# A bidirectional RWKV-7 and short-convolution layer on one core: operands stored in pairs, one convolution group done later, and the inverse's blocks stored from another queue

## The chip, the core and the metric

The kernel runs on one core of a Trainium2 chip. The metric is device time in microseconds (us) of one execution; before the change it is 1746.37 us, the median of three runs (1745.83 to 1748.89).

## What is computed

One layer for 128 context tokens and 2048 latent tokens (2176 columns) of width 1024, all in fp32. Both kinds of token go through a modulated RMS norm `h`, one input projection to eight groups of 512 channels, a mixer with two halves, and an output projection with a residual:

```python
proj = h @ lp['w_in']
r, k, v, g_a, b_gate, c_gate, u_conv, g_b = jnp.split(proj, IN_SPLITS, axis=-1)
ya, s_final = _wkv(h, r, k, v, s0, lp)                     # 8 heads x 64, two directions
ya = ya.astype(x.dtype) * jax.nn.silu(g_a)
yb = b_gate * _short_conv(c_gate * u_conv, lp['conv_w'], is_latent) * jax.nn.silu(g_b)
u = jnp.concatenate([ya, yb], axis=-1) @ lp['w_out']
```

`_wkv` is the RWKV-7 recurrence with a decay and an in-context rate for each direction:

```python
s_kk = jnp.einsum('bdhij,bdhj->bdhi', S, kk_t)
S = (S * w_t[..., None, :] - s_kk[..., :, None] * (kk_t * a_t)[..., None, :]
     + v_t[..., :, None] * k_t[..., None, :])
return S, jnp.einsum('bdhij,bdhj->bdhi', S, r_t)
```

## The kernel before

**Engines.** TensorE (PE) multiplies, VectorE (DVE), ScalarE (ACT) and GpSimd (POOL) work element by element, and SyncE (SP) issues nearly all transfers. A value that two phases share lies in a scratch tensor in memory (`scr_...` in the profile). The program gives the order of the steps, and a scheduler of the compiler, which works with times of its own, settles the order of the instructions on each engine.

**Phase 1** (`phase1`, from L43) makes everything that needs the projection. The columns are cut into six blocks of 384 columns (the last has 256), taken two by two, in thirds (`THIRD`). fp32 is split into a high and a low part, so a product `dense` of one block with 128 output channels is 24 matmuls (L160 to L162). In each third a loop over four groups `g` of 128 channels (L626 to L628) calls `turn(0, g, ...)` and `turn(1, g, ...)`, and each turn does both blocks of the third:

- The first turn does `mixA`: the products for k and r, the token shift (`shifted`: L319 and L321 on ScalarE, L323 on POOL, L327 or L329 on VectorE), the norm of kk by a sum over partitions (`part_sum`: L196, L197, L204, L205), and for both directions the decay (tanh, L371, and a scan, L375 or L377) and the four operands of the recurrence: `al` (L387), `rh` (L390), `kap` (L398) and `be` (L401 and L402). Each operand is a tile of 128x384 from a ring of four places with the tag `sp`, and is stored at once by SyncE (`spill`, L335) to `ops0` or `ops1`. A place is free again when its store has landed. A last sum over the heads, `psb`, gives `bsum`.
- The second turn does `gateA`: v, its transpose, centred, in `vt` (one place, L425 and L432) and stored (L433); the gate sg (L439, stored); and `q` (L441 to L444), which takes a place of the ring `sp`.
- Beside them a turn can do half of a convolution group (`partB`): `convB` with the products c and u (`mmc`, `mmu`) and the taps, or `gateB` with the products gb and b. In the first two thirds group g is done in the turns of g. In the last third groups 0 and 1 are spread over the four first turns, and groups 2 and 3 come after all mix turns, interleaved with `K.early()`.

Weights come in by `load_w` (L119): first from the input through a ring of two tiles `wr` of 4 KB a partition (used in the first third only, when the split parts are also stored), later as split parts.

**Phase 2** (`phase2`, from L694) is the recurrence, in chunks of 64 tokens and 17 stages of 16 chunk-heads. A stage s has these parts: `partL` loads operands into `rr` (L868, SyncE); `partM` copies block-diagonal operands (`bd`, L779, ScalarE), makes the products psF, psG (L892) with masks, and cuts the 32x32 diagonal blocks `dg`, which are stored to `at` (L899, on ScalarE's queue); `partI` loads them in another layout (`ab`, L914), inverts them on POOL (L919 to L934) and stores `zt` (L935, POOL's queue); `partW` loads `str`, `stl`, `sv` and the inverses `zc`; `partU` transposes them (`zr`, L984, VectorE) and completes the inverse (psU L992, psW); `partB` makes psX (L1018) and psE (L1029), E on VectorE (L1030); `partS` is the serial chain of states (psS L1054, sv L1067). M and the inverse of a stage run three stages ahead (`LA`). `K.early()` is the setup (among it `presetR`, L787, which writes an identity into `rr`) and L, M and I of stages 0 and 1. `main()` starts behind phase 1: it does M and I of stage 2, U and B of stage 0, and then the loop over the stages, in which the parts of coming stages are placed between the eight steps of the serial chain.

**Phase 3** is the output projection (psu, L1287 to L1289), partly ahead of the recurrence's end.

Of the kernel before, what the change touches and what calls it, by code (L numbers as in the profile page):

```python
# [6 lines left out]
F32 = mybir.dt.float32  # L7
# [20 lines left out]

OPS = dict(al0=0, rh0=1, ka0=2, be0=3, be1=0, ka1=1, rh1=2, al1=3)


class Ctx:
# [15 lines left out]
def phase1(K):  # L50
# [3 lines left out]
    wp = Pool(K, "p1w", "left", 2)  # L54
# [58 lines left out]
                up[n, d] = (hi[:, n, d], lo[:, n, d])  # L113

    kept = set()

    def load_w(cb):

# [212 lines left out]

    def spill(name, g, j, t_, nm):
        t0, n = BLK[j]
        dst = S[f"ops{name[2]}"][OPS[name]] if name in OPS else S[name]
        nc.sync.dma_start(dst[g * 128:(g + 1) * 128, t0:t0 + n], t_[:, :n])  # L335

    def mixA(g, j, ws, hh, lw, pre):

# [19 lines left out]
        for d in range(2):  # L358
            cs = slice(g * 128, g * 128 + 128)

            def lup(which):
                ps = pmm.tile([128, 384], F32, tag="mm", name=f"up{which}_{K.u()}")
                hi, lo = up[which, d]
                x = lw[which * 2 + d]
                T.matmul(ps[:, :n], hi[:, cs], x[:, :n], start=True, stop=False)
                T.matmul(ps[:, :n], lo[:, cs], x[:, :n], start=False, stop=True)
                return ps

            psw = lup(0)
            t = tl("t", 2)  # L370
            P.activation(t[:, :n], psw[:, :n], AF.Tanh, bias=dcol(D_W0H + d * 4 + g), scale=0.5)  # L371
            V.tensor_scalar(t[:, :n], t[:, :n], -0.5 * DEC, -0.5 * DEC, ALU.mult, ALU.add)
            c = t
            if d == 0:
                V.tensor_tensor_scan(c[:, :n], smask[:, :n], t[:, :n], 0.0, ALU.mult, ALU.add)  # L375
            else:
                V.tensor_tensor_scan(c[:, :n][:, ::-1], smask[:, :n], t[:, :n][:, ::-1], 0.0, ALU.mult, ALU.add)  # L377
            pt = rot(pp[d], "pp")
            c3 = c[:, :n].rearrange("p (a b) -> p a b", b=64)
            P.activation(pt[:, :nch, 1 - d:65 - d], c3, AF.Exp)  # L380
            P.activation(c[:, :n], c[:, :n], AF.Exp, bias=nln2[:], scale=-1.0)
            psa = lup(1)
            ta = tl("ta", 2)
            P.activation(ta[:, :n], psa[:, :n], AF.Tanh, bias=dcol(D_IBH + d * 4 + g), scale=0.5)
            v3 = lambda x_: x_[:, :n].rearrange("p (a b) -> p a b", b=64)
            al = tl("sp", 4)
            V.tensor_tensor(v3(al), v3(kk), pt[:, :nch, d:64 + d], ALU.mult)  # L387
            spill(f"al{d}", g, j, al, "al")
            rh = tl("sp", 4)
            V.tensor_tensor(v3(rh), v3(rS), pt[:, :nch, 1 - d:65 - d], ALU.mult)  # L390
            spill(f"rh{d}", g, j, rh, "rh")
            nc.scalar.dma_start(S[f"pc{d}"][g * 128:(g + 1) * 128, t0 // 64:t0 // 64 + nch], pt[:, :nch, 64 - 64 * d])

            kd = tl("kd", 2)
            P.activation(kd[:, :n], ta[:, :n], AF.Identity, bias=dcol(D_KA2 + g), scale=vcol(V_KA + g))
            V.tensor_tensor(kd[:, :n], kd[:, :n], kS[:, :n], ALU.mult)
            kap = tl("sp", 4)
            V.tensor_tensor(kap[:, :n], kd[:, :n], c[:, :n], ALU.mult)  # L398
            spill(f"ka{d}", g, j, kap, "kap")
            be = tl("sp", 4)  # L400
            V.scalar_tensor_tensor(be[:, :n], ta[:, :n], 1.0, kkn[:, :n], ALU.add, ALU.mult)  # L401
            V.tensor_tensor(be[:, :n], be[:, :n], c[:, :n], ALU.mult)  # L402
            spill(f"be{d}", g, j, be, "be")
            kds.append(kd)
        bs = kds[0]
        V.tensor_tensor(bs[:, :n], kds[0][:, :n], kds[1][:, :n], ALU.add)
# [6 lines left out]
    def gateA(g, j, ws, hh, bsum):  # L413
# [6 lines left out]
        psv = pax.tile([128, 3, 128], F32, tag="ax", name=f"psv{g}_{j}")  # L420
        for i in range(n // 128):
            T.transpose(psv[:, i, :], vS[:, i * 128:(i + 1) * 128], idt[:])
        vt = ta_.tile([128, 3, 128], F32, tag="vt", name=f"vt{g}_{j}", bufs=1)

        c0 = 1 if lat_off(j) else 0  # L425
        if c0:
# [11 lines left out]
        sg = tg  # L438
        V.scalar_tensor_tensor(sg[:, :n], tg[:, :n], 1.0, psg[:, :n], ALU.add, ALU.mult)  # L439
        spill("sg", g, j, sg, "sg")  # L440
        q = tl("sp", 4)  # L441
        V.tensor_tensor(q[:, :n], bsum[:, :n], vS[:, :n], ALU.mult)
        V.scalar_tensor_tensor(q[:, :n], q[:, :n], dcol(D_GBH + g), sg[:, :n], ALU.add, ALU.mult)
        spill("q", g, j, q, "q")  # L444
# [126 lines left out]
    for t3, js in enumerate(THIRD):  # L571
        wd, wi = wlora if t3 == 0 else (load_w(32), load_w(33))
        lws, pre, conv, sums = {}, {}, {}, {}
        more = coming(*THIRD[t3 + 1]) if t3 < 2 else iter(())
        WA, WB = ((4, 0), (8, 12)), ((20, 24), (28, 16))
        early = gate_rows() if t3 == 0 else iter(())
# [10 lines left out]
        def turn(h, ga, gb):  # L587
# [5 lines left out]
            for j in js:  # L593
# [13 lines left out]
                if ga == 3 and h and j == js[0] and t3 < 2:  # L607
                    run(more)
                    j2 = THIRD[t3 + 1][1]
                    more = make_h(j2, xb[j2])  # L610
            if first:
                wb = [load_w(cb + gb[0]) for cb in WB[gb[1]]]
                for j in js:
                    partB(gb[0], j, gb[1], wb)
# [9 lines left out]
            prepare(js[1])  # L624
            load_up()
        for g in range(4):  # L626
            turn(0, g, (g, 0) if t3 < 2 else (g // 2, g % 2))
            turn(1, g, (g, 1) if t3 < 2 else None)  # L628
        run(more)
        if t3 == 2:  # L630
            for p in (pax, ta_, hr, ca):
                p.close()
            early = K.early()
            for g in (2, 3):
                for h in range(2):
                    wb = [load_w(cb + g) for cb in WB[h]]
                    for j in js:
# [53 lines left out]
def phase2(K):  # L691
# [179 lines left out]
    def partM(s, st):  # L871

        at = S["at"][s]
        for gi, g in enumerate(st.g):
# [20 lines left out]
            def blocks():  # L895
                dg = tl([128, 8, 32], "dg", 1, O.rI)
                P.activation(dg[:], g.GA[:, :, 64:96], AF.Identity, scale=B.hm[:, 0:1])
                V.scalar_tensor_tensor(dg[:], g.GA[:, :, 96:128], B.hm[:, 1:2], dg[:], ALU.mult, ALU.add)
                nc.scalar.dma_start(at[gi * 8:gi * 8 + 8].rearrange("u s b j i -> (s b j) u i"), dg[:])  # L899

            F = lambda h: product(h, g.F, pb, rr[:, 2:4], B.msk[:, MF[d]], "F")
            GA = lambda h: product(h, g.GA, qb, rr[:, 1::-1], B.mkg[:, MG[d]], "G")
# [511 lines left out]
```

## Time and profile before

| | before |
|---|---|
| median of the runs | 1746.37 us (1745.83 to 1748.89) |
| span of the profiled execution | 1752.9 us |
| busy: PE, PEld, DVE, ACT, POOL | 94%, 89%, 62%, 50%, 33% |
| mean of PE's granted clock in the first third, second third, third 3, recurrence | 0.97, 0.98, 1.00, 0.96 |
| moved by DMA | 335.69 MB, 192 GB/s |

The median is of runs of their own; the profile is of one execution, 6.5 us longer. All durations are from that one. In a row of a timeline stand the start in us, the duration in us, the engine, the line of the kernel, the operation, what it writes and reads, and in brackets how long its engine stood idle before it and what ended that. In a row of the waits stand the engine and its tile and line, what it waited for, the us in total, how many times, and the longest. "Landing" is the time from a transfer's issue to its end.

Phase 1 fills the span up to about 1000 us (the first third from 60, the second from 395, the third's mix turns from 720 to 935, its late conv groups to 1002), the recurrence runs to about 1505 us.

### The profile page before, as it was taken

Reading aid. Unit: us, or ns where it says so; the run is one execution under the profiler, and the core shown is the slowest. Engines: PE = TensorE matmul, PEld = TensorE weight load, DVE = VectorE, ACT = ScalarE, POOL = GpSimd, SP = SyncE. Lnnn points to the kernel's source line nnn. Section 1 sums busy time; section 2 is a strip of 40 time slices with the busy share of each in tenths; the row PEclk is TensorE's granted clock in tenths of the full one; section 3 lists DMA queues with packets and bytes.
Section 4 is the critical chain, followed back from the end, with each engine's and each line's share of the span. In section 5 each row is a group of like instructions: output and inputs, shape, how many; then the busy total and the mean of one; then the engine's idle time right before and its main releaser. Section 6 shows DMA issues by size and latency. Waiting matters only on the chain. (4 is left out here: it accounts for less than half of the span.)

```text
span 1752.9 us, 33041 instructions
## 1 busy us (share of the span) xinstructions
PE 1647.9 (94%) x12400; PEld 1558.8 (89%) x12400; DVE 1093.0 (62%) x2092; ACT 870.1 (50%) x1719; POOL 582.1 (33%) x1089
## 2 busy tenths in 40 slices
PE   5999899998999999999998989999999999899998
PEld 2889898998999998999998979899999999787886
DVE  5875788866567766567764544475776666656333
ACT  4534455534143433334442367687788787633222
POOL 0011111111011101011120587777777778223221
PEclk9899999999999999999999998899999999999999
DMA  9797778785557646477666585587677875746442
GB/s 367 208 234 220 233 241 246 232 255 151 148 160 227 169 147 174 135 258 217 195 214 225 173 196 135 141 192 187 174 198 189 191 185 120 180 151 206 151 144 90
DMA packets 315825, 335.69 MB, mean 192 GB/s; under 512 B 166985, under 2 KB 263881, under 8 KB 301585
## 3 DMA queue, kind: packets, MB, share of 16 engines
q1 hardware_dynamic: 243360, 324.52, 62.6%
q10 hardware_dynamic: 70944, 4.60, 2.9%
q0 software_dynamic: 1360, 4.46, 0.7%
q8 instruction: 98, 1.61, 0.4%
q14 instruction: 63, 0.51, 0.1%
HBM read 221.42 MB, written 112.08 MB: 190 GB/s over the span
## 5 line engine op out<-in xcount | busy, mean ns | idle before, releaser
L934 POOL TENSOR_TENSOR zt<-zt,ztmp 128x30 f32<-128x30 f32 (+7 forms) x510 | 197.3, 387 | 39.3
L1054 PE MATMUL psS<-sv,E 128*128 128x64 f32 x1088 | 155.1, 277 | 1.0 <-DVE sv L1067 0.6
L1029 PE MATMUL psE<-str,stl 128*128 128x128 f32 x1088 | 144.1, 281 | 11.3 <-DVE E L1030 7.0
L1054 PEld LDWEIGHTS psS<-sv,E 128*128 128x128 f32 x1088 | 145.4, 200 | 3.3 <-DVE sv L1067 0.8
L1029 PEld LDWEIGHTS psE<-str,stl 128*128 128x128 f32 x1088 | 131.8, 194 | 14.1 <-DVE E L1030 7.9
L931 POOL TENSOR_TENSOR ztmp<-ab,zt 128x60 f32<-128x60 f32 (+7 forms) x255 | 130.8, 513 | 19.2
L1067 DVE TENSOR_TENSOR sv<-psS,pc 64x128 f32<-64x128 f32 x254 | 69.2, 277 | 92.9 <-PE psS L1054 92.2
L779 ACT COPY bd<-rr 64x512 f32<-64x512 f32 x136 | 84.0, 617 | 75.7 <-DMA rr<-scr_ops 23.3
L323 POOL TENSOR_TENSOR shk<-rawl 128x384 f32<-128x384 f32 (+1 forms) x24 | 20.7, 861 | 291.9 <-ACT rawl L319 291.9
L1030 DVE TENSOR_TENSOR E<-psE,msk 128x512 f32<-128x512 f32 x136 | 92.7, 684 | 33.0 <-PE psE L1029 32.3
L892 PE MATMUL psF<-rr,bd 128*128 128x128 f32 x544 | 80.0, 295 | 16.2 <-ACT Q L779 9.8
L892 PEld LDWEIGHTS psF<-rr,bd 128*128 128x128 f32 x544 | 70.7, 203 | 20.4 <-ACT Q L779 12.9
L1350 POOL TENSOR_TENSOR z<-z,x 128x512 f32<-128x512 f32 x32 | 43.6, 1364 | 126.6 <-DVE z L1346 105.9
L1018 PE MATMUL psX<-F,zb 128*128 128x128 f32 x544 | 78.2, 297 | 3.2 <-ACT zb L777 2.3
L197 POOL TENSOR_TENSOR hslb<-kd,hshb 128x384 fp32r<-128x384 f32 (+1 forms) x24 | 26.7, 1113 | 164.0 <-ACT hshb L196 143.5
L160 PE MATMUL mmc<-h,w 128*128 128x384 f32 (+1 forms) x192 | 67.9, 354 | 13.4 <-ACT q1r L321 9.8
L323 POOL TENSOR_TENSOR shv<-rawl 128x384 f32<-128x384 f32 (+1 forms) x24 | 25.4, 1060 | 153.4 <-ACT rawl L319 153.4
L892 PE MATMUL psG<-rr,bd 128*128 128x128 f32 x544 | 72.0, 280 | 4.4 <-DVE F L893 4.4
L1018 PEld LDWEIGHTS psX<-F,zb 128*128 128x128 f32 x544 | 71.6, 209 | 4.0 <-POOL zt L934 1.9
L892 PEld LDWEIGHTS psG<-rr,bd 128*128 128x128 f32 x544 | 65.7, 193 | 5.0 <-DVE F L893 4.8
L161 PE MATMUL mmc<-h,w 128*128 128x384 f32 (+1 forms) x192 | 66.1, 344 | 0.0
L162 PE MATMUL mmc<-h,w 128*128 128x384 f32 (+1 forms) x192 | 65.7, 342 | 0.0
(307 smaller groups left out, 5205.4 us busy)
## 6 DMA issues: line engine op xcount, KB each, us to landing
w<-scr_wsp SPq DMA_DIRECT2D x68, 1024.0 KB, 7.3
scr_wsp<-w SPq DMA_DIRECT2D x34, 1024.0 KB, 6.0
rr<-scr_ops SPq DMA_DIRECT2D x64, 512.0 KB, 4.6
scr_ops<-sp SPq DMA_DIRECT2D x160, 192.0 KB, 5.2
wr<-in_win SPq DMA_DIRECT2D x34, 512.0 KB, 6.3
ab<-scr_at SPq DMA_DIRECT2D x34, 256.0 KB, 4.2
x<-in_x SPq DMA_DIRECT2D x17, 512.0 KB, 3.8
wadas<-in_wada SPq DMA_DIRECT2D x8, 1024.0 KB, 13.0
```

Of the source, the lines that this page charges most:

```text
L160: T.matmul(ps[:, :n], w[:, 0, k], hh[:, 0, k, :n], start=k == 0, stop=False)
L161: T.matmul(ps[:, :n], w[:, 0, k], hh[:, 1, k, :n], start=False, stop=False)
L162: T.matmul(ps[:, :n], w[:, 1, k], hh[:, 0, k, :n], start=False, stop=k == 7)
L779: (V.tensor_copy if k in ON_DVE else P.copy)(dst, src)
L892: T.matmul(ps[:, i, :].rearrange("p (a b) -> p a b", b=64), w[:, u, :], x[:, :, u, :], start=True, stop=True)
L931: G.tensor_tensor(tv, ab[:, j:j + 2, j + 2:32].unsqueeze(1).broadcast_to((128, kn, 2, n)), zt[:, :kn, j:j + 2].unsqueeze(3).broadcast_to(( ...
L934: G.tensor_tensor(zt[:, :kn, j + 2:32], zt[:, :kn, j + 2:32], tv[:, :, r], ALU.subtract)
L1018: T.matmul(px[:, i, :], B.zb[:, gi, us.start + i, :], g.F[:, us.start + i, :], start=True, stop=True)
L1029: T.matmul(pe[:, i, hd, :].rearrange("p (b t) -> p b t", b=2), g.lt[:, :, hd, us.start + k + i].rearrange("p b t -> p (b t)"), g.rt[:, :, ...
L1030: V.tensor_tensor(g.E[n][:, k:k + 2].rearrange("p a b c -> p (a b) c"), pe[:].rearrange("p a b c -> p (a b) c"), B.msk[:, ME[g.d]].unsquee ...
L1054: T.matmul(sp[gi][:, q, hd, :], g.E[n][:, k, hd, :], sv[:, u, hd, :], start=True, stop=True)
L1067: r = V.tensor_tensor(dst, sp[gi][0:64, q], B.pc[0:64, d, 2 * p:2 * p + 2, c:c + 1].broadcast_to((64, 2, 64)), ALU.mult)
```

## The change

It has four parts. The lines of the kernel after are 11 to 13 further on than those of before.

1. **Pairs.** `al` and `rh` are written into the two halves of one tile, `kap` and `be` into those of another, and each pair is stored by one transfer (`spill2`): 96 stores for 192. In the first third the pairs have two places in the room of the former four. From the second third on, when `wr` has no weights to hold any more, every other pair lies in `wr`: four pair places.
2. **q and vt.** `q` is computed in `bsum` and takes no operand place. From the second third on `vt` lies in `wr` too, with two places.
3. **Convolution.** In the last third only group 0 is done beside the mix turns, its halves at g = 1 and g = 3; the first turns of g = 0 and g = 2 have none. Group 1 is done behind the mix turns with 2 and 3, interleaved with `K.early()` (which ends the pools for the operands first).
4. **The inverse's blocks.** `dg` is stored by SyncE (`D` is `nc.sync.dma_start`) in place of ScalarE.

```diff
@@ spill, new pair() and spill2()
 def spill(name, g, j, t_, nm):
     t0, n = BLK[j]
-    dst = S[f"ops{name[2]}"][OPS[name]] if name in OPS else S[name]
-    nc.sync.dma_start(dst[g * 128:(g + 1) * 128, t0:t0 + n], t_[:, :n])
+    nc.sync.dma_start(S[name][g * 128:(g + 1) * 128, t0:t0 + n], t_[:, :n])
+npair = [0]
+def pair():
+    npair[0] += 1
+    nm = f"pair{npair[0]}"
+    if late and npair[0] % 2:
+        return wp.tile([128, 2, 384], F32, tag="wr", name=nm, bufs=2)
+    return ta_.tile([128, 2, 384], F32, tag="sp", name=nm, bufs=2)
+def spill2(d, k, g, j, t_):
+    t0, n = BLK[j]
+    nc.sync.dma_start(S[f"ops{d}"][k:k + 2, g * 128:(g + 1) * 128, t0:t0 + n].rearrange("k p t -> p k t"), t_[:, :, :n])
@@ mixA
-al = tl("sp", 4)
+ar = pair()
+al, rh = ar[:, d], ar[:, 1 - d]
 V.tensor_tensor(v3(al), v3(kk), pt[:, :nch, d:64 + d], ALU.mult)
-spill(f"al{d}", g, j, al, "al")
-rh = tl("sp", 4)
 V.tensor_tensor(v3(rh), v3(rS), pt[:, :nch, 1 - d:65 - d], ALU.mult)
-spill(f"rh{d}", g, j, rh, "rh")
+spill2(d, 2 * d, g, j, ar)
...
-kap = tl("sp", 4)
+kb = pair()
+kap, be = kb[:, d], kb[:, 1 - d]
 V.tensor_tensor(kap[:, :n], kd[:, :n], c[:, :n], ALU.mult)
-spill(f"ka{d}", g, j, kap, "kap")
-be = tl("sp", 4)
...
-spill(f"be{d}", g, j, be, "be")
+spill2(d, 2 - 2 * d, g, j, kb)
@@ gateA
-vt = ta_.tile([128, 3, 128], F32, tag="vt", name=f"vt{g}_{j}", bufs=1)
+vt = (wp if late else ta_).tile([128, 3, 128], F32, tag="wr" if late else "vt", name=f"vt{g}_{j}", bufs=2 if late else 1)
...
-q = tl("sp", 4)
+q = bsum
@@ the loop over the thirds
+if t3:
+    late.append(t3)
...
-    if first:
+    if first and gb:
...
 for g in range(4):
-    turn(0, g, (g, 0) if t3 < 2 else (g // 2, g % 2))
+    turn(0, g, (g, 0) if t3 < 2 else {1: (0, 0), 3: (0, 1)}.get(g))
     turn(1, g, (g, 1) if t3 < 2 else None)
...
     early = K.early()
-    for g in (2, 3):
+    for g in (1, 2, 3):
@@ partM, blocks()
-nc.scalar.dma_start(at[gi * 8:gi * 8 + 8].rearrange("u s b j i -> (s b j) u i"), dg[:])
+D(at[gi * 8:gi * 8 + 8].rearrange("u s b j i -> (s b j) u i"), dg[:])
```

Three places show what it does to the order of the instructions. The names are `name_number<-what it reads`; numbers differ between the two kernels.

VectorE in the second third, group 3, block 3, from the first direction's last operands to the second's; `sp_3_3` and `pair..` are operand places, `pp0` and `pp1` the decays of the two directions. Before:

```order
L396 TENSOR_TENSOR kd_3_3_723_6356<-kd_3_3_723_6356,ok_701_6256 128x384
L350 TENSOR_SCALAR sq_3_3_702_6258<-pss3_3_6264 128x384
L387 TENSOR_TENSOR sp_3_3_712_6318<-kk_3_3_703_6269,pp0_0_472 128x384
L390 TENSOR_TENSOR sp_3_3_713_6321<-or_707_6302,pp0_0_472 128x384
L351 RECIPROCAL sq_3_3_702_6258<-sq_3_3_702_6258 128x384
L398 TENSOR_TENSOR sp_3_3_715_6328<-kd_3_3_714_6325,t_3_3_709_6307 128x384
L355 TENSOR_TENSOR sq_3_3_702_6258<-kk_3_3_703_6269,sq_3_3_702_6258 128x384
L480 TENSOR_TENSOR pv3_3_6430<-ct3_3_6402,mmu_728_6404 128x384
L406 TENSOR_TENSOR kd_3_3_714_6325<-kd_3_3_714_6325,kd_3_3_723_6356 128x384
L401 SCALAR_TENSOR_TENSOR sp_3_3_716_6331<-ta_3_3_711_6316,sq_3_3_702_6258 128x384
L387 TENSOR_TENSOR sp_3_3_721_6349<-kk_3_3_703_6269,pp1_0_473 128x384
```

The same stretch after:

```order
L401 TENSOR_TENSOR pair61_6184<-kk_3_3_569_6135,pp0_0_472 128x384
L402 TENSOR_TENSOR pair61_6184<-or_573_6168,pp0_0_472 128x384
L408 TENSOR_TENSOR kd_3_3_583_6216<-kd_3_3_583_6216,ok_567_6122 128x384
L401 TENSOR_TENSOR pair63_6211<-kk_3_3_569_6135,pp1_0_473 128x384
L402 TENSOR_TENSOR pair63_6211<-or_573_6168,pp1_0_473 128x384
L411 TENSOR_TENSOR pair62_6192<-kd_3_3_578_6189,t_3_3_575_6173 128x384
L363 TENSOR_SCALAR sq_3_3_568_6124<-pss3_3_6130 128x384
L411 TENSOR_TENSOR pair64_6219<-kd_3_3_583_6216,t_3_3_580_6200 128x384
L417 TENSOR_TENSOR kd_3_3_578_6189<-kd_3_3_578_6189,kd_3_3_583_6216 128x384
L364 RECIPROCAL sq_3_3_568_6124<-sq_3_3_568_6124 128x384
L418 SCALAR_TENSOR_TENSOR kd_3_3_578_6189<-kd_3_3_578_6189,dv_115,or_573_6168 128x384
```

The operands of the second direction have moved up beside those of the first, since each has a place of its own, and the reciprocal of the norm has moved behind them.

ScalarE from the last products of `K.early()` to the first copy of `main()`: `Q11` and `dg` belong to stage 1's M, `ct` and `sgb` with the group's number to the convolution, `bd0` to stage 2's M. Before:

```order
L779 COPY Q11_9277<-psQ1_1_9688 128x512
L899 DMA scr_at_65<-dg_1104_9684 128x8x32
L508 ACTIVATE sgb3_4_9907<-mmgb_1117_9882 128x384
L508 ACTIVATE sgb3_5_9966<-mmgb_1119_9941 128x256
L779 COPY bd0_9278<-rr1_9283 64x8x64 x2
```

After:

```order
L792 COPY Q11_8822<-psQ1_1_9226 128x512
L910 ACTIVATE dg_876_9222<-GA11_8821,hm_8809 128x256
L519 ACTIVATE sgb2_4_9445<-mmgb_889_9420 128x384
L519 ACTIVATE sgb2_5_9504<-mmgb_891_9479 128x256
L466 COPY ct3_4_9566<-mmc_895_9541 128x384
L466 COPY ct3_5_9626<-mmc_897_9601 128x256
L519 ACTIVATE sgb3_4_9691<-mmgb_901_9666 128x384
L519 ACTIVATE sgb3_5_9750<-mmgb_903_9725 128x256
L792 COPY bd0_8823<-rr1_8828 64x8x64 x2
```

Between stage 1's block and `main()` stood half a convolution group; now one and a half stand there. The block's store has left this queue.

SyncE in a stage of the recurrence, between two loads of `rr1` and the next load of `ab`; `stl` and `str` are loads of `partW`. Before:

```order
L868 DMA rr1_9283<-scr_ops1_59 128x2x512
L846 DMA stl0_10034<-scr_ops0_57 64x4x64 x2
L843 DMA str0_10040<-scr_ops0_57 64x2x256
L843 DMA str1_10041<-scr_ops1_59 64x2x256
L846 DMA stl1_10035<-scr_ops1_59 64x4x64 x2
L868 DMA rr1_9283<-scr_ops1_59 128x2x512
L914 DMA ab_1301_13890<-scr_at_65 64x1024 x2
```

After:

```order
L881 DMA rr1_8828<-scr_ops1_59 128x2x512
L859 DMA stl0_9818<-scr_ops0_57 64x4x64 x2
L856 DMA str0_9824<-scr_ops0_57 64x2x256
L856 DMA str1_9825<-scr_ops1_59 64x2x256
L859 DMA stl1_9819<-scr_ops1_59 64x4x64 x2
L912 DMA scr_at_65<-dg_1077_13495 128x8x32
L881 DMA rr1_8828<-scr_ops1_59 128x2x512
L927 DMA ab_1085_13674<-scr_at_65 64x1024 x2
```

The second direction's block is now stored between the loads of `stl1` and of `rr1`, ahead of the load that fetches it back; the first direction's stands before the load of `rr0` in the same way.

More of the change, by code (lines that the diff above doesn't have):

```diff
@@ L27 @@
 ND = 68
-OPS = dict(al0=0, rh0=1, ka0=2, be0=3, be1=0, ka1=1, rh1=2, al1=3)
 class Ctx:
@@ L115, in phase1 @@
     kept = set()
+    late = []
     def load_w(cb):
```

## The prediction

> **What bounds the kernel now.** The head of the page comes first: the span, and the busy share of TensorE.
>
> ```profile
> span 1752.9 us, 33041 instructions
> PE 1647.9 (94%) x12400; PEld 1558.8 (89%) x12400; DVE 1093.0 (62%) x2092; ACT 870.1 (50%) x1719; POOL 582.1 (33%) x1089
> ```
>
> TensorE (PE) is busy for 94% and the change takes no matmul away, so it can only win idle time of PE and time that PE spends at a low clock. The profiled span lies 6.5 us above the median of 1746.37 us (1745.83 to 1748.89); I sum differences against the span and subtract them from the median. About 0.2%, 3.5 us, is what a measurement here can tell from no change. Next the view of busy time by stretch: the first third of phase 1, the second, and the mix turns of the third. Columns: stretch, its length, busy time of PE, PEld, DVE, ACT, POOL (with counts), granted clock, DMA share, GB/s.
>
> ```profile
> 60.00:395.00 335.00, 317.51 (x1733) 300.87 (x1732) 250.18 (x443) 151.70 (x286) 44.89 (x42) 0.97 0.80 236
> 395.00:720.00 325.00, 310.09 (x1750) 306.78 (x1749) 204.69 (x371) 116.93 (x235) 41.95 (x42) 0.98 0.59 172
> 720.00:935.00 215.00, 211.38 (x1437) 209.49 (x1436) 138.38 (x277) 83.03 (x189) 37.07 (x48) 1.00 0.66 203
> ```
>
> PE idles 17.5, 14.9 and 3.6 us in them. Third 3 has next to nothing to win, and something to lose; what else can be won sits behind it, around 940 us and at the start of the recurrence, which PE's timeline shows below.
>
> **Second third: the places for operands.** The timeline of PE shows its four largest gaps there (the bracket is the idle time ahead and its releaser), and two 25-us stretches the clock around them.
>
> ```profile
> 432.88 0.69 PE L160 MATMUL mmc<-h,w 128*128 128x384 f32 x1 [4.87 <-ACT q1r L321]
> 517.45 0.44 PE L160 MATMUL mmc<-h,w 128*128 128x384 f32 x1 [2.54 <-ACT q1r L321]
> 593.08 0.45 PE L160 MATMUL mmc<-h,w 128*128 128x384 f32 x1 [1.77 <-ACT q1r L321]
> 688.71 0.66 PE L204 MATMUL psb<-hshb,onr 128*128 128x384 f32 x1 [3.38 <-ACT hshb L196]
> 500.00:525.00 25.00, 22.46 (x119) 22.14 (x119) 19.52 (x37) 12.99 (x26) 3.62 (x4) 0.93 0.61 160
> 575.00:600.00 25.00, 23.23 (x134) 22.91 (x133) 20.66 (x39) 13.51 (x28) 4.09 (x4) 1.00 0.64 154
> ```
>
> The gaps sum to 12.6 us. A clock of 0.93 over 25 us is 3.5 us at half clock, 1.7 us lost; the 2.54-us gap was followed by that, the 1.77-us gap was not. With 1.7 us each behind the three long gaps the prize is 12.6 + 5 = 18. [...] What starts the gaps is the view of VectorE's waits in the second third:
>
> ```profile
> DVE sp L398 <- DMA scr_ops<-sp: 9.4, 4, 3.6
> DVE sp L387 <- DMA scr_ops<-sp: 8.6, 2, 6.7
> DVE sp L401 <- DMA scr_ops<-sp: 5.6, 4, 2.3
> ```
>
> VectorE stands 23.6 us in ten waits for one of four operand places, while ScalarE's chain to the next matmul waits behind it. In the change a turn of a block writes four pairs into four pair places, so a place is taken again only a whole block later (about 40 us: 325 us hold eight such turns of a block), against landings of a few us. These waits go. Late next is the wait for tanh and for POOL's shift in the same turns, so not all 18 come back: I take −15, with ends −19 and −5.
>
> **First third.** Here there are two pair places with the bytes of the former four, and the second direction's al/rh waits for the first's. The largest of four rows of VectorE's waits for a place, and the landing time of the stores:
>
> ```profile
> DVE sp L387 <- DMA scr_ops<-sp: 17.3, 6, 5.0
> DMA to landing us min/median/max: 1.8/4.9/13.5
> ```
>
> A pair place needs both halves landed, and both halves are issued at the later one's time; but half as many stores queue on SP. The first makes places come free later, the second lets stores land sooner, and I see neither outweigh the other: 0. The ends are the 17.3 us of waits in PE's 17.5 of idle time, a third of them won (−6) or half as much again added (+8).
>
> **Third 3: moving conv group 1 out.** A conv group is 4 products for the 384- and the 256-column block; PE's starts give a product's length:
>
> ```profile
> 925.82 0.33 PE L160 MATMUL mmu<-h,w 128*128 128x384 f32 x1
> 929.98 0.28 PE L160 MATMUL mmc<-h,w 128*128 128x256 f32 x1
> 932.85 0.28 PE L160 MATMUL mmu<-h,w 128*128 128x256 f32 x1
> ```
>
> 4.16 us and 2.87 us, so 4 × 7.03 = 28 us move behind the mix turns, with their loads; PE does them anyway: 0 by itself. A turn (k, r, v, g) without conv holds the same 28 us of dense products, and about 4 us of small ones: 32. Two of the four turns, g = 0 and 2, now have no conv. VectorE was busy 138.4 us in this stretch; the seven lines of the two conv groups (largest and smallest shown) sum to 13.8, the two of lora (larger shown) to 7.2:
>
> ```profile
> L464 DVE SCALAR_TENSOR_TENSOR ob<-rawl,dv,ob 128x384 f32<-128x384 f32 (+1 forms) x4 | 2.7, 686 | 0.0
> L83 DVE TENSOR_SCALAR ob<-rawl,dv 128x384 f32<-128x384 f32 (+1 forms) x4 | 1.5, 379 | 0.0
> L562 DVE TENSOR_TENSOR lw<-lf,lw 64x384 fp32r<-64x384 f32 (+1 forms) x8 | 4.6, 570 | 0.3
> DVE t L372 <- ACT t L371: 14.1, 4, 3.6
> DVE sp L401 <- DMA scr_ops<-sp: 13.9, 7, 2.9
> DVE sp L387 <- DMA scr_ops<-sp: 11.4, 4, 3.3
> ```
>
> 117.4 / 4 = 29.4 us of VectorE a turn, against 32 of PE: PE has little left to run ahead with. The 25.3 us of waits for places (the last two rows) go with the new places, the 14.1 for tanh stay. I charge one gap of 1.77 us, without a fall of the clock, for each of the four blocks of these two turns: +7, ends 0 (VectorE keeps up) and +26 (rival 1).
>
> **Start of the early part.** PE stands here once, for the first load of rr, whose tile is preset behind the last vt store:
>
> ```profile
> 935.80 0.76 DVE L787 COPY rr<-I 128x512 f32<-128x512 f32 x2 [6.72 <-DMA scr_vt<-vt]
> 943.16 1.19 PE L892 MATMUL psF<-rr,bd 128*128 128x128 f32 x4 [5.88 <-DMA rr<-scr_ops]
> 925.00:950.00 25.00, 19.12 (x118) 18.83 (x116) 9.27 (x21) 4.56 (x8) 0.00 (x0) 0.86 0.85 299
> ```
>
> The gap costs 5.88 us and, at 0.86, 25 × 0.14 = 3.5 us of clock. vt moves to wr, so the preset no longer waits 6.72 us for its store; but the load still waits for the last operand stores, which stay where they were. I take −5, ends −8.5 and 0.
>
> **Start of the recurrence.** The first inverse begins when its block has come back from memory; its result feeds U, and PE's first psU waits for it:
>
> ```profile
> 981.06 0.20 POOL L923 COPY dgp<-ab 128x16 f32<-128x16 f32 x1 [57.71 <-DMA ab<-scr_at]
> 1008.92 0.76 POOL L935 DMA_DIRECT2D scr_zt<-zt  x1 [0.31 <-POOL zt L934]
> 1017.43 0.76 PE L992 MATMUL psU<-zr,GA 32*32 32x32 f32 x36 [2.79 <-DVE zr L984]
> 1157.19 0.98 PE L992 MATMUL psU<-zr,GA 32*32 32x32 f32 x50
> 1253.37 0.81 PE L992 MATMUL psU<-zr,GA 32*32 32x32 f32 x39
> 1342.95 1.20 PE L992 MATMUL psU<-zr,GA 32*32 32x32 f32 x64
> ```
>
> The inverse takes POOL 27.9 us (981.06 to 1008.92). At the start the stages are slower than that and than later ones: four stages from 1017.43 to 1157.19 are 139.8 us, three later ones 89.6, 29.9 each. The first four lose 139.8 − 119.6 = 20 us, and 2.8 ahead of the first. With 28 us more conv work in front, and the inverses started at the same distance behind the mix turns, POOL is one inverse ahead when the recurrence begins. I take −20, ends −25 and −8 (the lead is used up by a POOL no faster than PE).
>
> **The block store on SyncE.** On ScalarE's queue it is issued as soon as its data is there; on SyncE it stands behind the stl loads, ahead of rr and of its own load back, ab. A steady stage, and the page's row for the load of the block (KB each, us to landing):
>
> ```profile
> 1282.42 1.26 SPq L846 DMA_DIRECT2D stl<-scr_ops  x2
> 1282.98 0.37 ACTq L899 DMA_DIRECT2D scr_at<-dg  x1
> 1286.25 1.10 SPq L914 DMA_DIRECT2D ab<-scr_at  x2
> 1255.69 0.60 POOL L935 DMA_DIRECT2D scr_zt<-zt  x1 [0.30 <-POOL zt L934]
> 1272.62 0.69 DVE L984 STREAM_TRANSPOSE zr<-zc 128x512 f32<-128x512 f32 x1
> ab<-scr_at SPq DMA_DIRECT2D x34, 256.0 KB, 4.2
> ```
>
> Its issue costs ScalarE 0.37 us, and SyncE holds rr back until dg is computed: 0.7 to 2.5 us a stage, from the distance of these SPq rows. From zt's store to its use are 16.9 us; less two trips through memory of about 4.2 us, 8.5 are slack, which covers that. I take +3 for the first stages without slack, ends −3 and +10.
>
> Sum: −15 + 0 + 7 − 5 − 20 + 3 = −30. 1752.9 becomes 1723, and 1746.4 becomes 1716.
>
> **The rivals.**
>
> 1. VectorE binds the conv-less turns: each of the four blocks pays a whole gap like that at 432.88 with its clock, 4.87 + 1.7 = 6.6, 26 in all and 19 more than charged: 1735. For it: 29.4 against 32; against it: PE lost only 3.6 us in this third beside 25.3 us of waits for places. Chance 0.17.
> 2. The pace of the inverse falls away in the later stages too, and the early gap goes entirely: −25, −8.5 and −19 at the ends, 1716 − 5 − 3.5 − 4 = 1703. Chance 0.10.
> 3. Slower: the block store, in SyncE's line, lands late. It decides once landing and line come to more than the 8.5 us of slack. With the longest landing of an operand store, 13.5 instead of 4.2, and 2.5 in line it is 11.8 later, 3.3 past the slack. The way from the store (1282.98) to its use two stages on (1272.62 + 2 × 29.9 = 1332.4) is 49.4 us, 1.65 stages, so 14 stages hold 8.5 such gaps of 3.3, each with 1.7 of clock: +43, less the +3 charged, 1756. Against it: the store is small, and its load back lands in 4.2. Chance 0.07. [...]
> 4. The new places do nothing and the moved conv is paid back by the pace of the inverse: 1746. Chance 0.06.
>
> **How the numbers follow.** The forecast, 1716, has 0.60, its own range 1702 to 1731. The range 1700 to 1741 leaves out rivals 3 and 4 and the tails. Faster: 0.59 + 0.16 + 0.10 = 0.85; same: 0.06; slower: 0.07 and the tails of the forecast and of rival 1, 0.09.
>
> **What would show it.** In the profile after: the sp waits gone in the second third and its gaps at mmc with them; PE's idle share in third 3 up by 7 us, at the two turns without conv (by 26, and rival 1 is right); no wait for vt ahead of the rr preset; the first four psU near 30 us apart. The forecast is wrong if POOL's wait for ab grows by more than 8.5 us a stage, or if the pace of the first stages stays at 35 us.

## The result and the profile after

The kernel after takes 1733.15 us, the median of six runs (1726.64 to 1738.91), against 1747.63 us for the kernel before (1745.32 to 1752.42, six runs). The ratio is 0.9905 with a 95% interval of 0.988 to 0.993: 16.6 us less, where 30 were forecast. It lies inside the range of 1700 to 1741 and just outside the forecast's own 1702 to 1731, and the sign was right. The term of the store was wrong by 10 us and that of the start of the recurrence by 9; other terms made up for a part. Rival 1's number, 1735, is 2 us off, but its mechanism is not what happened: that is chance.

The head of the page of the kernel after:

```profile
span 1724.9 us, 32848 instructions
PE 1640.9 (95%) x12400; PEld 1556.2 (90%) x12400; DVE 1107.3 (64%) x2092; ACT 868.8 (50%) x1719; POOL 587.4 (34%) x1089
```

This profiled execution is the shortest of its six (1726.64), while the profiled one of before, 1752.9, is one of the longer ones. So the 28 us between the two spans overstate the change, and single stretches have to be read from several kernels. The stretches below begin and end at the same work in both: the first third to the first lora product of the second, the second third, third 3 to the last conv product, the first four stages of the recurrence (from the first psU to the fifth stage's), and the rest of the recurrence to the last psS (in the kernel before that is at 1588.6 us; the 1505 us given further up for the end of the recurrence is too early). Columns as before: length, busy time of PE, PEld, DVE, ACT, POOL, granted clock, DMA share, GB/s. The kernel before:

```profile
0.00:390.40 390.40, 353.73 (x1892) 323.61 (x1893) 291.11 (x539) 180.03 (x338) 46.16 (x57) 0.97 0.80 247
390.40:716.70 326.30, 311.39 (x1758) 308.08 (x1757) 204.69 (x371) 117.08 (x235) 41.95 (x42) 0.98 0.59 174
716.70:1002.60 285.90, 276.40 (x1896) 274.14 (x1895) 172.34 (x346) 102.65 (x224) 56.02 (x87) 0.99 0.65 203
1017.40:1157.20 139.80, 129.19 (x1437) 124.32 (x1438) 70.15 (x145) 102.27 (x192) 107.91 (x243) 0.91 0.64 159
1157.20:1588.60 431.40, 412.56 (x4693) 394.59 (x4692) 273.93 (x557) 315.85 (x602) 278.76 (x608) 0.97 0.72 177
```

The kernel after:

```profile
0.00:392.60 392.60, 352.61 (x1893) 322.65 (x1894) 290.65 (x539) 180.08 (x338) 44.38 (x57) 0.96 0.79 245
392.60:700.60 308.00, 305.55 (x1758) 304.20 (x1756) 210.06 (x371) 116.55 (x235) 42.18 (x42) 1.00 0.64 184
700.60:985.70 285.10, 278.22 (x1895) 276.12 (x1895) 182.44 (x346) 101.69 (x224) 85.91 (x146) 0.98 0.67 205
999.90:1130.60 130.70, 127.01 (x1437) 123.36 (x1437) 70.91 (x146) 102.25 (x192) 89.08 (x200) 0.91 0.67 167
1130.60:1560.70 430.10, 413.12 (x4692) 395.79 (x4692) 273.36 (x556) 316.08 (x602) 282.31 (x608) 0.96 0.72 178
```

The second third is 18.3 us shorter: PE idles 2.5 us in it in place of 14.9, at a clock of 1.00. The first four stages are 9 us shorter, not 20. The rest of the recurrence did not change in this pair of profiles; that the store costs there shows only over several.

### The profile page after: what moved, and what is told of

It is laid out like the page before. It is cut to its first block, busy times and chain, and to the rows that moved or that the text cites. A ratio compares the mean times of both kernels' runs of the same rounds, so it can differ in the third digit from the quotient of the medians.

```text
span 1724.9 us, 32848 instructions
## 1 busy us (share of the span) xinstructions
PE 1640.9 (95%) x12400; PEld 1556.2 (90%) x12400; DVE 1107.3 (64%) x2092; ACT 868.8 (50%) x1719; POOL 587.4 (34%) x1089
## 3 DMA queue, kind: packets, MB, share of 16 engines
q10 hardware_dynamic: 35584, 0.14, 1.3%
## 5 line engine op out<-in xcount | busy, mean ns | idle before, releaser
L905 PE MATMUL psF<-rr,bd 128*128 128x128 f32 x544 | 78.8, 291 | 13.0 <-ACT Q L792 10.6
L160 PE MATMUL mmgb<-h,w 128*128 128x384 f32 (+1 forms) x192 | 64.4, 335 | 0.4 <-ACT q1r L321 0.4
```

The lines of the kernel that those rows point to most:

```text
L160: T.matmul(ps[:, :n], w[:, 0, k], hh[:, 0, k, :n], start=k == 0, stop=False)
L905: T.matmul(ps[:, i, :].rearrange("p (a b) -> p a b", b=64), w[:, u, :], x[:, :, u, :], start=True, stop=True)
```

## The experiments

All times are medians, with the ratio to the kernel before, timed beside it, and its 95% interval. "Four psU" is the stretch of the first four stages, "the rest" the one behind it. The four parts of the change make three switches: P (pairs, with q and vt), C (conv group 1 behind the mix turns) and S (the block store on SyncE). All eight combinations were run:

| kernel | P | C | S | time, us | ratio to before (95%) |
|---|---|---|---|---|---|
| before, timed beside each | | | | 1747.63 to 1752.06 | 1 |
| e5 | | | x | 1764.21 | 1.0062 (1.0039 to 1.0086) |
| e7 | | x | | 1750.16 | 0.9992 (0.9972 to 1.0013) |
| e3 | | x | x | 1762.35 | 1.0051 (1.0019 to 1.0084) |
| e6 | x | | | 1727.67 | 0.9860 (0.9839 to 0.9881) |
| e2 | x | | x | 1740.2 | 0.9938 (0.9914 to 0.9961) |
| e1 | x | x | | 1718.05 | 0.9818 (0.9789 to 0.9848) |
| after | x | x | x | 1733.15 | 0.9905 (0.988 to 0.993) |

**e1_store_back.** The kernel after, with the store on ScalarE's queue again:

```diff
-D(at[gi * 8:gi * 8 + 8].rearrange("u s b j i -> (s b j) u i"), dg[:])
+nc.scalar.dma_start(at[gi * 8:gi * 8 + 8].rearrange("u s b j i -> (s b j) u i"), dg[:])
```

> The kernel after with one edit: the inverse's blocks are stored by ScalarE's queue again. My account (the store costs 3 us in SyncE's line, within slack): 2 to 4 us less than the kernel after, about 1730. Rival (the store in SyncE's line is what ate half of the forecast gain): 10 us or more less, 1722 and below. Second rival (off ScalarE's queue it is a gain, a part of the shorter recurrence): 5 us or more above the kernel after, 1738 and more.

Measured: 1718.05 us (1713.71 to 1724.98), 15 us below the kernel after, with no run of the one within the runs of the other. My 3 us fell and the first rival held. It is the fastest kernel of the study.

**e2_conv_back.** The kernel after, with the conv loop and the list of groups behind it as before:

```diff
-turn(0, g, (g, 0) if t3 < 2 else {1: (0, 0), 3: (0, 1)}.get(g))
+turn(0, g, (g, 0) if t3 < 2 else (g // 2, g % 2))
-for g in (1, 2, 3):
+for g in (2, 3):
```

> The kernel after with one edit: conv group 1 of the last third is done beside the mix turns again. My account (28 us of work ahead of the recurrence hide the first inverses): the first four psU are again 135 to 140 us long, those of the kernel after are 131, and the time is 8 to 10 us above the kernel after, about 1742. Rival (the shorter start is chance or the store's doing, and the mix turns without conv lose what is won): the same time as the kernel after, 1733, with the first four psU near 131.

Measured: 1740.2 us, 6 to 7 above the kernel after (by the ratios and by the medians); four psU 140.0 us. The account held for the four psU; the total is a little under its 8 to 10, and the intervals of the two ratios overlap. Third 3 is 281.2 us here and 285.1 in the kernel after: by this pair, the turns without conv cost 4 us.

**e3_pairs_back.** The kernel before with the conv moved and the store on SyncE: both edits shown above, and no pairs.

> The kernel after with one part undone: operands, q and vt as in the kernel before, four places and a store for each. My account (the second third gained 18 us from places): the second third takes 326 us again and the time is 15 to 18 us above the kernel after, 1748 to 1751. Rival (VectorE's waits moved but the gaps are made by something else): within 5 us of the kernel after, 1733 to 1738.

Measured: 1762.35 us, 26 to 29 above the kernel after, and 9 above the kernel before. More than expected, since third 3 suffers as well: 296.6 us against 285.9 before.

**e4_before_again.** The kernel before, unchanged.

> The kernel before once more, for a second profile. If the profiled execution of before (span 1752.9) was a long one by chance and that of after (1724.9) a short one, this span is near 1745, and the stretches that differ from the first profile name where executions vary: I expect the recurrence, by half-clock windows, and phase 1 within 2 us. If executions vary everywhere, no stretch repeats within 2 us.

Measured: 1751.35 us, the median of eight runs, ratio 1.0006 (0.998 to 1.0031); the profiled span is 1746.9. The stretches repeat within 1.1 us to the end of the first four stages; the rest of the recurrence is 422.2 us in place of 431.4. So these two executions differ by the recurrence behind its start, as expected, and a difference of some us there means nothing in a single pair of profiles.

**e5_store_alone.** The kernel before, with the store on SyncE only.

> The kernel before with one edit: the inverse's blocks are stored by SyncE. Account A (the block's place in SyncE's line costs, whatever stands in phase 1): 10 to 18 us above the kernel before, 1760 to 1768, and all of it between the first psU and the last psS. Account B (the 15 us between the kernel after and the one with the store back come from the order that the scheduler makes of that one program): within 4 us of the kernel before, either sign.

Measured: 1764.21 us, ratio 1.0062: 11 us above before. With e1, e2 and e6, e3 and e7 there are four pairs for the store: 15, 14, 10 and 11 us by the ratios, whatever stands in phase 1. Account A holds, B is out. Four psU are 139.3 us as before; the cost is in the rest, 444.1 us:

```profile
1157.10:1601.20 444.10, 418.52 (x4692) 400.23 (x4692) 274.77 (x557) 316.89 (x604) 282.19 (x616) 0.95 0.69 172
```

**e6_pairs_alone.** The pairs with q and vt on the kernel before.

> The kernel before with pairs, q and vt as in the kernel after, conv and store as before. If the store's cost adds to the rest (account A): some 15 us below the kernel with the conv back (1740), 1725; second third near 273 us, start of the recurrence (four psU) near 137. Account B: within 5 us of 1740.

Measured: 1727.67 us; the second third is 309.7 us, 273.7 of them from its first psb (the 273 of the expectation); four psU 136.7. The pairs alone win 24 us, and the account of an additive store holds.

**e7_conv_alone.** The conv edit of e2, the other way, on the kernel before.

> The kernel before with the conv group moved, places and store as before. Account A: some 15 us below the kernel with the pairs back (1762), 1747: third 3 with the conv groups behind it is 10 us longer than before's 286 (turns without conv that wait for places), the first four psU 10 to 16 us shorter than 140. Account B: 1758 and more. Rival on the conv (the turns without conv cost nothing by themselves): third 3 within 3 us of before, and 1740 or less.

Measured: 1750.16 us, no change (0.9972 to 1.0013). Third 3 is 295.6 us, 9.7 longer than before, and four psU are 128.4, 11 shorter: given back in the same kernel. PE's timeline of e7 shows two of the gaps, in turns without conv, each of them a wait for what VectorE or ScalarE makes:

```profile
763.64 0.39 PE L204 MATMUL pss<-hshs,onr 128*128 128x256 f32 x1 [1.67 <-ACT hshs L196]
780.37 0.53 PE L422 MATMUL psv<-idt,ov 128*128 128x128 f32 x2 [2.44 <-DVE ov L329]
```

In VectorE's own list a wait of 2.98 us for an operand place ends at 761.84, ahead of the first, and one of 4.78 at 777.10, ahead of the second.

**e8_pair_places_single_stores.** e1, with a store for each half of a pair:

```diff
+spill2(d, 2 * d, d, g, j, ar)
 V.tensor_tensor(v3(rh), v3(rS), pt[:, :nch, 1 - d:65 - d], ALU.mult)
-spill2(d, 2 * d, g, j, ar)
+spill2(d, 2 * d, 1 - d, g, j, ar)
... (the same for kap and be; spill2 stores one half)
```

> The kernel after with the store back on ScalarE's queue, and each half of a pair stored by its own transfer as soon as it is written: the same places, 192 stores as before. If the places make the gain: the same as that kernel, 1718 within 4, second third near 273. Rival (half as many stores in SyncE's line make it): 8 us or more above, second third over 280.

Measured: 1721.59 us (1719.44 to 1724.7), ratio 0.9826 (0.9804 to 0.9848) against e1's 0.9818. In the total there is no difference that can be told. The second third is 277.8 us from its first psb, in e1 274.2; that lies between the 273 and the 280 of the two accounts. In whole the second third is 313.8 us, against 326 to 330 without the change of places: the places make most of its gain, and the halved number of stores may be worth some 4 us of it (one profile).

**e9_store_behind_rr.** The kernel after, with both blocks stored at the head of `partI`, behind the next loads of rr in program order, and two `dg` places:

```diff
-D(at[gi * 8:gi * 8 + 8].rearrange("u s b j i -> (s b j) u i"), dg[:])
...
 def partI(s, st):
+    for gi, g in enumerate(st.g):
+        D(at[gi * 8:gi * 8 + 8].rearrange("u s b j i -> (s b j) u i"), g.dg[:])
```

> The kernel after with the inverse's blocks still stored by SyncE, but both behind the next loads of rr (two dg places). Theory (the store ahead of rr makes rr late, ScalarE's copies late, and PE stands at psF behind psU, where its clock then falls): the store's cost goes, 1717 to 1723; psF's waits for ScalarE in the steady stages near 6 us in place of 8.5, time at half clock in the recurrence back from about 70 us to about 43. Rival (any further transfer in SyncE's line costs, wherever it stands): 1730 to 1736, with waits and clock as in the kernel after.

Measured: 1736.06 us (1731.82 to 1742.98), at the upper end of the rival's 1730 to 1736. But the run does not decide between the two. Each store now stands behind one direction's load of rr and still ahead of the other direction's, and the waits that the edit was to shorten grew, ScalarE's for rr to 7.7 us from 5.6 in the kernel after, and PE's at psF to 11.2 from 8.1 (from 1130 to 1480 us):

```profile
ACT bd L792 <- DMA rr<-scr_ops: 7.7, 5, 2.6
PE psF L905 <- ACT Q L792: 11.2, 16, 2.4
```

**e10_filler_matmuls.** The kernel after, with matmuls into a place that is overwritten before it is read:

```diff
 pw = O.p2.tile([128, 16, 32], F32, tag="s", name=f"psW{s}")
+for _ in range(3):
+    T.matmul(pw[:].rearrange("p a b -> p (a b)")[:, 0:256], B.idt[:], B.mkg[:].rearrange("p a b -> p (a b)"), start=True, stop=True)
```

> The kernel after with three matmuls of 128x256 that no one reads, placed behind psU ahead of psF in each stage (some 0.66 us a stage, 11 us in all where PE has no gap for them). Theory (the clock falls when a window between psU and psW holds too little work of PE): falls behind psU become rare, time at half clock in the recurrence under 30 us in place of 55 to 80, and the total is not above the kernel after's 1733: 1722 to 1731. Rival (the falls come of the wait alone, or by chance): half clock as before, and 1738 to 1745.

Measured: 1727.27 us (1724.97 to 1733.06), 0.9863 (0.9833 to 0.9893) beside the after's 0.9905 (0.988 to 0.993): more work, and 6 us less by the medians, with intervals that overlap by a little. The windows from the first psU to the last psS:

```profile
1001.10:1126.50 125.40, 122.71 (x1460) 118.80 (x1460) 71.70 (x145) 102.41 (x192) 86.27 (x193) 0.99 0.71 174
1126.50:1559.00 432.50, 416.82 (x4771) 397.04 (x4770) 275.15 (x557) 315.51 (x602) 284.96 (x615) 1.00 0.73 177
```

The theory held. The clock is 0.99 and 1.00 where it was 0.91 and 0.96. The trace has 7 us at half clock in these two stretches, against 55 in the kernel after. The fillers cost more than my estimate of 0.66 us a stage (the stretch without gaps and falls, a fall counted as half its time, grew by 23 us, 1.4 a stage), so what the clock won was nearly paid back in work.

**e11_first_third_singles.** e1, with one operand a store in the first third, and pairs only behind it: one tile of four places for the whole of phase 1, every second pair of which lies in `wr` from the second third on.

```diff
-return ta_.tile([128, 2, 384], F32, tag="sp", name=nm, bufs=2)
+i = npair[0] // 2 % 2 if late else npair[0] % 2
+return spt[:, 2 * i:2 * i + 2]
...
+spt = ta_.tile([128, 4, 384], F32, tag="sp", name="spt", bufs=1)
... (in the first third each half is stored as soon as it is written)
```

> The kernel after with the store back on ScalarE's queue, and in the first third four places of one operand with a store each, as before; pairs only from the second third on. If the pair places cost in the first third (profiles show 392 to 395 us to its end, against 390 to 391.5 before): 2 to 4 us below that kernel's 1718, about 1715, first third near 391. Rival (the difference there is the clock's chance): 1718, no difference.

Measured: 1728.87 us, 11 above e1, first third 398.7 us. The expectation failed; in that profile the first third alone had 44 us at half clock, as in e1. Third 3 and the first four stages are longer too (288.5 and 127.7 us, in e1 282.8 and 123.7), for which the run gives no reason. Whether pair places cost in the first third stays open.

**e12_small_store_in_line.** e1, with a second, tiny store in SyncE's line:

```diff
 nc.scalar.dma_start(at[gi * 8:gi * 8 + 8].rearrange("u s b j i -> (s b j) u i"), dg[:])
+D(S["dum"][s, gi], dg[0:1, 0, :])
... (and the scratch tensor dum)
```

> The kernel with the store back on ScalarE's queue (1718), and besides it a store of 32 elements of dg that no one reads, issued by SyncE at the place in its line where the kernel after has the block's store. It adds the wait for dg and the issue to SyncE's line, and next to no bytes. Theory (SyncE's line itself is the cost: what stands behind it, rr above all, comes late by about 1 us, and PE's wait at psF tips the clock): 1728 to 1736; ScalarE's waits for rr in the steady stages 5 us or more in place of 2, time at half clock in the recurrence 50 us or more in place of 27. Rival (the block's bytes in SyncE's ring, or the time that ScalarE no longer spends on it and the other order that follows): 1716 to 1722, waits and clock as without it.

Measured: 1722.24 us (1718.14 to 1724.49), 0.9833 (0.9803 to 0.9862). That is nearer to e1 than to the kernel after, and its interval holds e1's ratio but not the after's. By the medians, the wait for dg and the issue in SyncE's line are 4 us of the 15, which the intervals do not tell from none.

## Why the prediction was right or wrong

Its terms, each from the profiles that have the part and those that have not (lengths in us, one profile for each kernel; e10 and e11 are left out where their own edit lies in the stretch, and e12 counts as without S; the difference is of the means):

| term | forecast | without | with | measured |
|---|---|---|---|---|
| second third, P | −15 | 326.3, 327.2, 328.4, 329.8, 327.6 | 308.0, 310.3, 310.3, 309.7, 313.8, 309.9, 308.7, 309.7, 308.8 | −18 |
| first third, P | 0 | 390.4, 391.5, 390.3, 387.9, 390.9 | 392.6, 394.8, 392.3, 392.6, 394.8, 395.8, 394.7, 391.6 | +3 |
| third 3 with the early part, P and C | +7 − 5 | 285.9, 286.8, 285.8 | 285.1, 282.8, 282.0, 286.1, 283.4, 288.5, 284.7 | −2 |
| four psU, C | −20 | 139.8, 139.4, 139.3, 140.0, 136.7 | 130.7, 123.7, 131.4, 128.4, 130.5, 124.5, 127.7, 127.8 | −11 |
| rest of the recurrence, S | +3 | 431.4, 422.2, 426.1, 423.1, 436.1, 421.1, 425.1, 429.3 | 430.1, 439.8, 439.3, 444.1, 446.0 | +13 |

**The second third** went as the prediction had it, and gave the whole prize of 18 that the prediction had counted before it took off 3. Its ten waits for places are gone from VectorE's list, which now begins with the tanh that was named as next (PE idles 2.5 us in all beside it); the first third keeps a large row for pairs:

```profile
DVE t L385 <- ACT t L384: 21.6, 8, 3.6
DVE ok L329 <- POOL shk L323: 16.3, 4, 4.5
```

```profile
DVE pair L401 <- DMA scr_ops<-pair: 29.2, 9, 4.9
```

29.2 us in nine waits there, about as much as the 26.4 in 14 of before. That the reason is mostly the places and not the number of stores is shown by e8. Pairs, q and vt were changed together in every run, so the share of each is not known. The two places in `wr` serve `vt` too, so they are taken again sooner than the prediction's whole block; no wait for them shows.

**The first third** is 3 us longer by the table, but e11, with single places there, is 398.7, so this is not shown to come from the pairs.

**Third 3.** The two conv-less turns make the stretch 4 us longer with pairs (e2 to the kernel after, e6 to e1: 281.2 to 285.1, 278.7 to 282.8), inside the 0 to 26 of the prediction. Without pairs the same move costs 10 (e3, e7). So rival 1, in which a conv-less turn leaves PE waiting, is nearer to what happens when the waits for places are still there. The wait for rr ahead of the first psF fell from 5.88 us to this:

```profile
896.93 1.45 PE L905 MATMUL psF<-rr,bd 128*128 128x128 f32 x8 [2.02 <-DMA rr<-scr_ops]
```

**The start of the recurrence** gained 11, not 20: in the kernel after the first stages are 31.1 to 34.9 us apart. The prediction put the whole 20 down to POOL, which would be "one inverse ahead when the recurrence begins". Two things in this were wrong. POOL is ahead for stages 0 and 1 only; the third inverse needs M of stage 2, which `main()` makes behind the conv groups, and POOL ran dry. Rows of POOL's timeline, of VectorE's, and of PE's waits from 985 to 1131 us, all of the kernel after:

```profile
1019.09 0.20 POOL L936 COPY dgp<-ab 128x16 f32<-128x16 f32 x1 [24.30 <-DMA ab<-scr_at]
1077.47 0.60 POOL L948 DMA_DIRECT2D scr_zt<-zt  x1 [0.30 <-POOL zt L947]
```

```profile
1056.61 0.71 DVE L997 STREAM_TRANSPOSE zr<-zc 128x512 f32<-128x512 f32 x1 [1.70 <-DMA zc<-scr_zt]
...
1085.38 0.69 DVE L997 STREAM_TRANSPOSE zr<-zc 128x512 f32<-128x512 f32 x1
```

```profile
PE psU L1005 <- DVE zr L997: 1.8, 1, 1.8
```

The lead is gone by stage 3 (7.9 us from the store of its inverse at 1077.47 to its transpose at 1085.38, against 36 to 40 for the first two). But little waits for it any more: VectorE stands 1.70 us for stage 2's inverse and not at all for stage 3's, where before it stood 9.1 us in three of these stages, and PE waits for zr only ahead of the first psU. What is left of the 20 is the step that the prediction left out, PE's clock. Before, PE idled 10.6 us in the four stages and ran at half clock for 24, which by an estimate costs some 12 us, half of it. In the kernel after it idles 3.7 us and still runs at half clock for 24. In e1, where POOL ran dry for 22.1 us as well, the clock was 0.99 and the four stages took 123.7:

```profile
1001.60:1125.30 123.70, 118.47 (x1438) 115.04 (x1438) 72.84 (x144) 100.41 (x188) 84.57 (x191) 0.99 0.72 177
```

e8, which has the same places, conv order and queue for the store, ran at half clock for 24 us there and took 130.5. Over the profiles of the table's row, moving the conv group took the idle time from a mean of 8.9 to 4.3 us and the time at half clock from 27.3 to 15.3.

**The store** is the wrong term: +13 in place of +3. The prediction costed it as a delay of the inverse, found 8.5 us of slack and called it covered. The slack was there: the way from zt's store to zr's transpose is 11 to 20 us in the kernel after's stages from 4 on. The price came by another road, PE's clock. In the rest of the recurrence PE waits at psF, behind psU, for ScalarE's list of copies. Two rows each, of e1 and of e5 (waits from 1130 to 1480 us):

```profile
ACT bd L792 <- DMA rr<-scr_ops: 1.9, 3, 0.8
PE psF L905 <- ACT Q L792: 6.3, 16, 1.3
```

```profile
ACT bd L779 <- DMA rr<-scr_ops: 7.1, 3, 3.3
PE psF L892 <- ACT Q L779: 9.1, 16, 1.9
```

In this stretch PE's wait is 5.1 to 7.0 us in the eight profiles with the store on ScalarE's queue and 8.0 to 11.2 in the five with it on SyncE. It grows by 3 us in all between e1 and e5, which would be little, but it grows in single stages past 1 us, and then the clock falls for the work behind it. The timeline of the kernel after at stage 12, and the same time cut in pieces of 3.41 us:

```profile
1374.61 1.20 PE L1005 MATMUL psU<-zr,GA 32*32 32x32 f32 x64
1375.74 1.19 PE L1067 MATMUL psS<-sv,E 128*128 128x64 f32 x8
1378.55 1.82 PE L905 MATMUL psF<-rr,bd 128*128 128x128 f32 x8 [1.63 <-ACT Q L792]
1380.30 0.31 PE L1012 MATMUL psW<-zc,bu 32*32 32x32 f32 x2
1380.54 1.11 PE L1067 MATMUL psS<-sv,E 128*128 128x64 f32 x4
1381.59 1.91 PE L1012 MATMUL psW<-zc,bu 32*32 32x32 f32 x62
```

```profile
1372.08:1375.49 3.41, 3.41 (x79) 3.29 (x80) 1.91 (x5) 2.63 (x6) 2.95 (x6) 1.00 0.83 187
1375.49:1378.90 3.41, 1.78 (x32) 1.59 (x26) 1.87 (x5) 3.29 (x8) 2.96 (x6) 1.00 0.68 143
1378.90:1382.31 3.41, 3.41 (x41) 3.00 (x41) 0.28 (x1) 2.01 (x4) 2.75 (x9) 0.50 1.00 233
1382.31:1385.72 3.41, 3.41 (x55) 3.35 (x50) 1.03 (x2) 1.18 (x2) 1.79 (x5) 0.50 0.43 133
1385.72:1389.14 3.42, 3.42 (x17) 3.42 (x18) 1.57 (x3) 1.13 (x2) 3.21 (x7) 0.50 0.50 156
```

A piece in which PE is busy for 1.78 of 3.41 us is followed by three at half clock, the first two of which hold the 32x32 matmuls of psW: behind the 1.63-us wait 5 us more are lost, by an estimate (half of the 10.24 us of the three). In 13 profiles (all but that with the fillers), stages 4 to 13 are 130 in all. In 94 PE waited at psF for ScalarE for under 0.8 us or not at all: no fall of the clock, and a mean length of 30.2 us. In 28 it waited 1 us or more: 21 with a fall, and 34.6 us (8 lie between, 2 with a fall). With the store on ScalarE's queue 12 of 80 stages had such a wait, with it on SyncE 16 of 50. That the clock is what makes these stages long is supported by e10; that SyncE's store makes the waits at psF more frequent is counted here. Of the 13 us of the term, time at half clock in the rest of the recurrence goes from a mean of 24.8 to 45.7 us, which by an estimate is some 10 (half of it), and PE's idle time from 15.4 to 21.0; the two overlap. Single profiles overlap as well: e7, without the store, has 44.4 us at half clock, the kernel after 30.7.

How the store makes PE wait longer at psF is not settled. Its wait and issue in SyncE's line (e12) are not the whole of it. That it makes rr late stays a candidate, since e9 did not take it out of rr's way: ScalarE's waits for rr from 1130 to 1480 us are 5.6 to 7.7 us in four of the five profiles with the store on SyncE, 2.0 in the fifth (e3), and 0.5 to 2.7 in the eight others. Left are also the block's own bytes in SyncE's queue (1040 packets a store, from the packets that left ScalarE's queue: 70944 before, 35584 after, 34 stores) and the 0.4 us that ScalarE no longer spends on the issue, with the order that follows. The runs do not tell these apart.

The store did not land late on SyncE: its median landing from 1130 to 1480 us is 3.0 us in the kernel after and 4.5 in e9, both on SyncE, against 4.3 on ScalarE's queue in e1. Rival 3 had the sign of the store's cost (+43 there, +13 measured), but built it on a late landing, which no run shows.

**The sum.** The five measured terms give −15, the runs −16.6. The three parts other than the store were forecast at −33; their stretches give −28, and the runs of e1 −32 (0.9818 of 1750.5). The −20 was too large by 9, the pairs did 3 to 4 us more than their terms in the second and the last third each, and the first third took 3 back. That −33 and −32 lie so near is in part luck.

## What to carry to other kernels

Ask of each moved transfer not only whether its data has slack, but what on the engine that is the bound will wait a microsecond longer, and what the clock does behind that wait; here some 3 us of waits were worth 13. Run the parts of a bundle apart: of these, one won 24 us by itself, one won 6 to 10 only where the first was present, and one lost 10 to 15 in every company. With more places for a result in flight, a reordering that made its stretch 10 us longer made it 4 us longer.

## What the runs showed of the hardware

The low clock, 0.50, was granted in pieces of 3.41 us on a fixed grid (the last low stretch of a trace, at its end, aside): the rows above are cut on it, and in each of the 14 profiles all low stretches begin at the same residue of 3.413 us, to 0.02 us. No idle piece stands ahead of the fall in those rows: PE was busy for 1.78 of the 3.41 us just before it.

Cut on that grid, the recurrence of the 14 profiles (from the first psU to the last psS) tells more. Of the pieces at full clock with PE busy under half the time, 26 of 27 were followed by half clock, of those at 0.5 to 0.9 busy 60 of 276, of those from 0.9 up to less than full 0 of 339. Once at half clock, with PE busy throughout, 76 of the 84 pieces that held some of the 32x32 matmuls of psU and psW were followed by another at half clock, of the 87 without them 6. So a wait just ahead of psW was dear.

A wait's price therefore also hangs on how the grid lies to it: of the 28 waits of 1 us or more counted above, all 13 that left PE busy for 0.58 of a piece or less had a fall, and 8 of the 15 others; one of 1.50 us that lay across two pieces had none. That the spread of the kernel after, 12 us in six runs, comes from this is likely and not shown. With matmuls without use (e10, of the form 128*128 128x256) the clock was 0.99 and 1.00: 23 us of such work won 24 us of clock, by an estimate (half of the 48 us at half clock that went), and 2 of gaps in the profile. A smaller dose was not tried.
